# The second layer's z projection by Strassen's form, box sums as jobs through DRAM, and some moved steps

## The chip, the cores and the metric

The kernel runs on one core of a Trainium2 chip. The metric is the device time of one execution in microseconds (us); three runs of the kernel before give a median of 2036.6 (2034.02 to 2039.65). A core has five engines that work from queues of their own, each in order: TensorE (PE, matmuls), VectorE (DVE), ScalarE (ACT), GpSimd (POOL) and SyncE (SP, which only starts transfers). POOL starts transfers too.

## The reference, cut to what matters

Two layers over 1024 tokens of width 1024, with a context of 256 tokens. Layer 0 is a bidirectional mLSTM mixer, layer 1 a grid pooling mixer. Each is: norm, modulate, mixer, norm of the output, gated residual. Layer 1's mixer:

```python
def pool_mixer(h, grid, w_in, w_pool, pool_scale, w_out):
    u, z = jnp.split(h @ w_in, 2, axis=-1)          # 2048 each
    ...
    for g, w in enumerate(POOL_WINDOWS):            # 2, 4, 8, 16
        xg = ug[:, :, g, :]
        ...
        m = box_mean(box_mean(x2, w, 2), w, 1)...   # 16 x 64 grid
        diffs.append(m - xg)
    d = jnp.stack(diffs, axis=2).astype(h.dtype)
    y = jnp.einsum("btgi,gio->btgo", d, w_pool).reshape(bsz, t, D_INNER) * pool_scale
    return (y * jax.nn.silu(z)) @ w_out
```

## The kernel before

Everything lies with features on partitions and tokens along the row. A matrix of weights comes in tiles of 128 output features (`load_w`, L138): SP loads 512 KB, ACT rounds it to a high part, DVE subtracts that for a low part. A product in near full precision is three matmuls per block of 128 inputs (`mm3`, L147: high x high, high x low, low x high), each 128 x 512.

Layer 0 first makes features (`features`, `token_part`, 16 tiles), in which v is formed in small matmuls whose results ACT copies (L415) and, five at a time, casts to a high part (L418) with a low part by DVE before POOL stores both. Then come the z and o tiles in pairs by Strassen's form (`strassen`, inside the block with the T tiles): the pair's weights and the layer input are each cut in 2 x 2 blocks; seven products of four blocks take the place of eight. POOL forms the four weight sums (L574 to L577), ACT and DVE split each product's weights (L584, L585), and DVE combines the results (L593). The sums of the input's blocks were formed earlier (`block_sums`) and lie in DRAM.

The attention heads follow. For the first head SP starts the loads of one x chunk (`start_head`), the gate rows (`load_gates`, L712, L705 asked together with `load_ctx_gates`), the other x chunks (`finish_x`), and the v parts (`fetch_v`); `make_A` and `next_q` form the first q (copied by ACT at L734), and `decay` turns gate rows into exponentials on ACT (L768 to L772).

After the heads come the output product of layer 0 in two halves of 512 tokens (`product`), with a norm of each half as a background job that is advanced by `tick` between the matmuls of other work (`norm0`, `residual`, `next_input`). `squares` lets ACT square a tile and POOL add it (L983); the sum goes through a PE column sum to the norm's factor. `residual` stores its tiles from POOL's queue (L1007).

Layer 1 goes group by group, g = 0 to 3, four u tiles, four z tiles and four pool tiles each. Group 0's u and z tiles run first for half 0, under the norm of half 1, and then for half 1. A u tile's result is copied by ACT twice, into a padded grid U (L1076) and a plain copy (L1077). `box` makes the sums over the window by doubling adds on DVE (L1089, L1093), scales, subtracts (L1097 to L1104), and splits the difference in high and low (L1106, L1107). A z tile gets Silu from PSUM (L1082) and stays in SBUF. A pool tile multiplies four differences by `bw_pool`; DVE scales by `pool_scale` and z (L1158); for groups 0 to 2 POOL stores y to DRAM. In groups 1 to 3 the tiles follow `ORDER_B`, so boxes lie between products. The last product reads y back.

PE's order is written out by hand from ctx1 to the end of group 0's halves, and again for the last product; the order on the other engines and on SP, and PE's order elsewhere, is set by a scheduler that simulates the program. SBUF tiles come from tagged pools: 32 tiles S4 of 4 KB a partition, five T5, six pt of 2 KB, two each of wr, wh, wl (weights raw, high, low). A tile is free again when all that read it, a store to DRAM too, has ended.

Of the kernel before, what the change touches and what calls it, by code (L numbers as in the profile page):

```python
# [51 lines left out]
def hybrid_block(ctx: ExitStack, tc: tile.TileContext, xT, ctxT, vecs, w_ada0, w_ada, w_blk, w_krow, blk_mask, w_gate, w_in, b_gate, w_out,  # L52
# [38 lines left out]
    def f(t):  # L91
        return t.bitcast(F32)
# [39 lines left out]
    x1_d = dr.tile([P, KD, T], F32, name="x1_d")  # L132
    y2_d = dr.tile([12, P, T], F32, name="y2_d")
# [261 lines left out]
    def token_part(n, xmh, xml, xch, xcl):  # L395

        bv = small1([P, 32, 4], "bv", 1)
        V.tensor_tensor(bv, mask, wb[:, 2, n:n + 1].to_broadcast([P, 32, 4]), op=ALU.mult)
        bv = bv.rearrange("p a b -> p (a b)")
        vv = small1([P, 2, 144], "vv", dt=F32R)  # L400
        V.tensor_copy(vv[:, 0, :P], bv)
        V.tensor_tensor(vv[:, 1, :P], bv, f(vv[:, 0, :P]), op=ALU.subtract)
        V.tensor_copy(vv[:, :, P:], f(gm_all[:, n]).rearrange("p (a b) -> p a b", a=2))
        for s0 in (0, 5):
# [12 lines left out]
            V.tensor_tensor(pre[:, s0:s0 + 5], pre[:, s0:s0 + 5], vst[:, 0, :, P:], op=ALU.add)  # L417
            S.activation(vhl[:, 0], vst[:, 0, :, :P], AF.Copy)  # L418
            V.tensor_tensor(vhl[:, 1], vst[:, 0, :, :P], f(vhl[:, 0]), op=ALU.subtract)
            for t, dst in ((vhl[:, 0], vh_d), (vhl[:, 1], vl_d)):  # L420
                nc.gpsimd.dma_start(dst[n // 4, :, s0:s0 + 5, (n % 4) * P:(n % 4 + 1) * P], f(t))
        yield

        gx = gx_all[:, n]
        for ci, (o, w) in enumerate(CHUNKS):
            ch, cl = (xch[0][:, o:o + w], xcl[0][:, o:o + w]) if ci < 2 else (xch[1], xcl[1])
            if n == 0:
                mm(gacc[ci][:32, :w], gx, ch, True, False)
# [106 lines left out]
    with ctx0:  # L535
# [29 lines left out]
        def strassen(src, done):  # L565


            r1, r2 = tl("wr", [P, 8, P]), tl("T5", [P, 8, P])
            nc.sync.dma_start(r1, src[0])
            nc.sync.dma_start(r2, src[1])  # L570
            a11, a12, a21, a22 = r1[:, :4], r1[:, 4:], r2[:, :4], r2[:, 4:]
            s12, s34 = tl("T5", [P, 2, 4, P]), tl("T5", [P, 2, 4, P])
            s1, s2, s3, s4 = s12[:, 0], s12[:, 1], s34[:, 0], s34[:, 1]
            G.tensor_tensor(s1, a21, a22, op=ALU.add)  # L574
            G.tensor_tensor(s2, s1, a11, op=ALU.subtract)
            G.tensor_tensor(s3, a11, a21, op=ALU.subtract)
            G.tensor_tensor(s4, a12, s2, op=ALU.subtract)  # L577
            wt = []

            def product(tag, a, b):  # L580
                i = len(wt) % 2
                wt.append((tl("wh", [P, 2, 4, P], F32R), tl("wl", [P, 2, 4, P], F32R)) if i == 0 else wt[-1])
                hi, lo = (t[:, i] for t in wt[-1])
                S.activation(hi, a, AF.Copy)  # L584
                V.tensor_tensor(lo, a, f(hi), op=ALU.subtract)  # L585
                p = pt_(tag)
                for k in range(4):
                    mm3(p, hi[:, k], lo[:, k], *b[k], k == 0, k == 3)
                return p

            def plus(p, t, d=None):
                d = tl("pt", [P, 512]) if d is None else d
                V.tensor_tensor(d, p, t, op=ALU.add)  # L593
                return d

            p = product("pa", a11, b11)
            p1 = tl("pt", [P, 512])
            S.activation(p1, p, AF.Copy)
            done(0, 0, plus(product("pc", a12, b21), p1))
            u2 = plus(product("pa", s2, tpart(2)), p1, p1)  # L600
            u3 = plus(product("pc", s3, tpart(3)), u2)
            p = product("pa", s1, tpart(1))
            done(1, 1, plus(p, u3))
            plus(p, u2, u2)
            done(1, 0, plus(product("pc", a22, tpart(4)), u3, u3))
            done(0, 1, plus(product("pa", s4, b22), u2, u2))

# [42 lines left out]
        for n in range(0, KE, 2):  # L650
            prod = strassen if n else plain
# [190 lines left out]
    def next_q(cur, tp):  # L842
        return make_q(cur["hd"], cur["A"], tp)
# [150 lines left out]
    def residual(yo, rs, o, w, xr, dst, acc2, engs):  # L994
# [5 lines left out]
        for n in range(8):  # L1000
# [5 lines left out]
            if n % per == per - 1:  # L1006
                nc.gpsimd.dma_start(dst[:, n - per + 1:n + 1, o:o + w], yo[n // per])  # L1007
# [11 lines left out]
    def next_input(x1, rs, hf):  # L1019
        for kp in range(4):  # L1020
            a, b = tl("S4", [P, 2, 512], F32R), tl("S4", [P, 2, 512], F32R)
            h2[hf, kp] = (a, b)
            for j in range(2):
# [4 lines left out]
                V.scalar_tensor_tensor(b[:, j], o, sh1[:, k:k + 1], f(a[:, j]), op0=ALU.add, op1=ALU.subtract)  # L1028
                yield STEP_N
# [31 lines left out]
    def u_start(g):  # L1061
# [4 lines left out]
        U = tl("T5", [P, R_, C_])  # L1066
# [3 lines left out]
        return U, tl("S4", [P, T]), R_, C_, r0, hw  # L1070

    def u_half(ut, w, hf):
        U, ur, R_, C_, r0, hw = ut
        p = pt_("pa")
        h2mm(p, w, hf)
        S.activation(U[:, r0 + 8 * hf:r0 + 8 * hf + 8, hw:], p.rearrange("p (r c) -> p r c", c=64), AF.Copy)  # L1076
        S.activation(ur[:, hf * 512:(hf + 1) * 512], p, AF.Copy)  # L1077

    def z_half(sz, w, hf):
        p = pt_("pc")  # L1080
        h2mm(p, w, hf)
        S.activation(sz[:, hf * 512:(hf + 1) * 512], p, AF.Silu)  # L1082

    def box(ut, g, imv):
        U, ur, R_, C_, r0, hw = ut
        win = WINDOWS[g]
# [18 lines left out]
        a, b = tl("S4", [P, T], F32R), tl("S4", [P, T], F32R)  # L1105
        S.activation(a, ur, AF.Copy)  # L1106
        V.tensor_tensor(b, ur, f(a), op=ALU.subtract)  # L1107
        return a, b

    yraw = {}  # L1110
    for g in range(4):
        imap = tl("T5", [P, T])
        nc.sync.dma_start(imap, inv_cnt[g:g + 1].to_broadcast([P, T]))
        imv = imap.rearrange("p (r c) -> p r c", c=64)
        ut, szs, d = [None] * 4, [None] * 4, []
        if g == 0:
            for hf in range(2):
                for j in range(4):
                    if hf == 0:
                        ut[j] = u_start(g)  # L1120
                    u_half(ut[j], load_w(bw_in[4 * g + j]), hf)
                    if hf:
                        d.append(box(ut[j], g, imv))
                for j in range(4):
                    if hf == 0:
                        szs[j] = tl("S4", [P, T])
                    z_half(szs[j], load_w(bw_in[KE + 4 * g + j]), hf)
                if hf == 0:
                    drain()
            ctx1.close()  # L1130

        def u_tile(j):
            w = load_w(bw_in[4 * g + j])
            ut[j] = u_start(g)
            for hf in range(2):
                u_half(ut[j], w, hf)

        def z_tile(j):
            w = load_w(bw_in[KE + 4 * g + j])
            szs[j] = tl("S4", [P, T])  # L1140
            for hf in range(2):
                z_half(szs[j], w, hf)

        def pool_tile(j):
            n = 4 * g + j
            w = load_w(bw_pool[n], 4)
            for hf in range(2):
                s_ = slice(hf * 512, hf * 512 + 512)
                p = pt_("pb")
                for k in range(4):  # L1150
                    mm3(p, w[0][:, k], w[1][:, k], d[k][0][:, s_], d[k][1][:, s_], k == 0, k == 3)
                if g < 3:
                    o = tl("pt", [P, 512])
# [4 lines left out]
                V.scalar_tensor_tensor(o, p, vc("pool_scale", n), szs[j][:, s_], op0=ALU.mult, op1=ALU.mult)  # L1158
                if g < 3:
                    nc.gpsimd.dma_start(y2_d[n, :, s_], o)  # L1160

        def box_tile(j):
            d.append(box(ut[j], g, imv))

        if g:
            for step in ORDER_B:
                dict(u=u_tile, b=box_tile, z=z_tile, p=pool_tile)[step[0]](int(step[1]))
        else:
            for j in range(4):
                pool_tile(j)  # L1170
# [115 lines left out]
```

## Time and profile before

| what | value |
|---|---|
| median of three runs | 2036.6 us (2034.02 to 2039.65) |
| profiled execution | 2035.27 us, span 2032.8 us |
| PE busy | 1970.0 us, 97% |
| DVE, ACT, POOL busy | 62%, 40%, 25% |
| DMA | 339.47 MB, mean 167 GB/s |
| mean granted clock of PE | 0.992 |

The profiled execution is one run of the program with the hardware profiler; its span goes from the first to the last instruction. Matmuls are pipelined, so two that follow each other overlap in the trace: the time of one is best read from a run of many. Time in which an engine stands still is put down to what released it last.

### The profile page before, as it was taken

What the parts mean: (1) busy time and instruction counts of PE and PEld (TensorE: products, weight loads), DVE (VectorE), ACT (ScalarE), POOL (GpSimd) and SP (SyncE); (2) the same over time, 40 slices, a digit from 0 to 9 for tenths busy, and PEclk for the clock granted to TensorE, in tenths of its full rate; (3) what the DMA queues carried; (4) which work ended last, traced back from release to release, by engine and by line L of the source; (5) the groups of instructions that cost most, each with busy time, mean ns of one, the idle gap of its engine ahead of it and who ended that gap; (6) DMA issues with size and microseconds to landing.
All of it is one profiled execution on the core that took longest, in us unless ns stands there. A gap on an engine that the chain in (4) does not pass through costs nothing.

```text
span 2032.8 us, 26908 instructions
## 1 busy us (share of the span) xinstructions
PE 1970.0 (97%) x10050; PEld 1661.2 (82%) x10050; DVE 1256.6 (62%) x2092; ACT 812.5 (40%) x1357; POOL 500.2 (25%) x682
## 2 busy tenths in 40 slices
PE   6899999999999899999999999999999999999997
PEld 4788888788888688888888878887888888888897
DVE  4777777777767567676576662544747292744444
ACT  5567777433333433323332232533423131224443
POOL 2144334354443111111111101524000000000285
PEclk9999999999999999999999999999999999999998
DMA  9377777854444746446363324534331312133473
GB/s 360 130 259 256 257 258 253 319 167 135 131 150 132 295 148 210 179 140 242 111 232 126 133 70 153 196 113 166 94 114 42 104 52 92 49 114 140 166 272 122
DMA packets 115986, 339.47 MB, mean 167 GB/s; under 512 B 13036, under 2 KB 20716, under 8 KB 115856
## 3 DMA queue, kind: packets, MB, share of 16 engines
q1 hardware_dynamic: 85824, 234.80, 34.2%
q0 software_dynamic: 30032, 102.96, 13.7%
q8 instruction: 78, 1.28, 0.3%
q14 instruction: 52, 0.43, 0.1%
HBM read 234.77 MB, written 102.94 MB: 166 GB/s over the span
## 4 chain that ended last, share of the span: by engine, by line
PE 89%; DMA 3%; ACT 3%; DVE 2%; POOL 2%; issue 1%; SPq 0%; POOLq 0%; DVEq 0%; ACTq 0%
PE pa L136 45%; PE pc L136 34%; PE pb L136 7%; PE pb L795 2%; POOL hn L983 1%; PE pc L826 1%; DVE S L915 1%; DMA S<-in_w_ada_dram 1%; DMA S<-in_ctxT_dram 0%; DMA cst<-in_w_blk_dram 0%; DMA S<-a_d 0%; DMA wr<-in_w_ada_dram 0%; DMA S<-in_xT_dram 0%; POOL S L1003 0%; ACT wh L142 0%
## 5 line engine op out<-in xcount | busy, mean ns | idle before, releaser
L136 PE MATMUL pa<-S,wh 128*128 128x512 f32 (+1 forms) x2448 | 703.5, 372 | 0.0
L136 PEld LDWEIGHTS pa<-S,wh 128*128 128x128 f32 x2448 | 433.9, 189 | 67.7
L136 PE MATMUL pc<-S,wh 128*128 128x512 f32 (+1 forms) x1664 | 465.3, 366 | 1.8 <-DVE wh L721 0.9
L136 PE MATMUL pa<-S,wl 128*128 128x512 f32 (+1 forms) x1224 | 449.9, 368 | 0.1
L136 PEld LDWEIGHTS pc<-S,wh 128*128 128x128 f32 x1664 | 301.3, 189 | 53.4 <-DVE S L915 1.5
L144 DVE TENSOR_TENSOR wl<-wr,wh 128x1024 fp32r<-128x1024 f32 (+1 forms) x124 | 150.2, 1211 | 264.4 <-ACT wh L142 263.2
L136 PE MATMUL pc<-S,wl 128*128 128x512 f32 (+1 forms) x832 | 302.6, 365 | 0.3 <-DVE wl L144 0.2
L142 ACT ACTIVATE wh<-wr 128x1024 fp32r<-128x1024 f32 (+1 forms) x124 | 124.7, 1006 | 365.1 <-PE pc L136 144.4
L136 PEld LDWEIGHTS pa<-S,wl 128*128 128x128 f32 x1224 | 230.5, 188 | 39.8 <-DVE wl L144 0.5
L136 PE MATMUL pa<-S,S 128*128 128x512 f32 (+1 forms) x1152 | 249.6, 363 | 8.0 <-ACT S L734 8.0
L136 PE MATMUL pc<-S,pt 128*128 128x512 f32 x960 | 227.6, 392 | 0.8 <-DVE pt L798 0.5
L136 PEld LDWEIGHTS pa<-S,S 128*128 128x128 f32 x1152 | 192.3, 190 | 37.3 <-ACT S L734 8.6
L136 PEld LDWEIGHTS pc<-S,pt 128*128 128x128 f32 x960 | 178.3, 188 | 37.8 <-DVE S L735 1.0
L136 PEld LDWEIGHTS pc<-S,wl 128*128 128x128 f32 x832 | 157.4, 189 | 26.0 <-DVE wl L144 0.8
L983 POOL TENSOR_TENSOR hn<-hn,pt 128x512 f32<-128x512 f32 (+1 forms) x48 | 75.7, 1578 | 284.4 <-ACT pt L982 283.5
L797 ACT ACTIVATE pt<-pb 128x512 fp32r<-128x512 f32 (+1 forms) x96 | 47.8, 524 | 221.6 <-PE pb L795 221.6
L754 DVE SCALAR_TENSOR_TENSOR T<-pa,T 128x256 f32<-128x256 f32 (+3 forms) x184 | 78.2, 455 | 32.7 <-PE pa L136 31.8
L584 ACT ACTIVATE wh<-T 128x512 fp32r<-128x512 f32 x70 | 41.2, 627 | 96.3 <-PE pc L136 79.5
L136 PE MATMUL pb<-S,wh 128*128 128x512 f32 x256 | 78.9, 389 | 0.0
L415 ACT ACTIVATE T<-pb 128x288 f32<-128x288 f32 x160 | 62.5, 413 | 40.5 <-PE pb L136 33.0
L808 DVE BATCH_NORM_STATS2 st<-pc 128x6 f32<-128x512 f32 x32 | 22.4, 699 | 86.6 <-PE pc L136 86.5
L144 DVE TENSOR_TENSOR wl<-T,wh 128x1024 fp32r<-128x1024 f32 x32 | 45.7, 1428 | 43.4 <-ACT wh L142 43.3
(344 smaller groups left out, 2591.5 us busy)
## 6 DMA issues: line engine op xcount, KB each, us to landing
wr<-in_bw_in_dram SPq DMA_DIRECT2D x40, 512.0 KB, 3.6
wr<-in_w_in_dram SPq DMA_DIRECT2D x34, 512.0 KB, 4.2
wr<-in_w_ada_dram SPq DMA_DIRECT2D x32, 512.0 KB, 4.2
wr<-in_w_out_dram SPq DMA_DIRECT2D x32, 512.0 KB, 3.6
T<-in_bw_out_dram SPq DMA_DIRECT2D x32, 512.0 KB, 4.0
S<-y_d SPq DMA_DIRECT2D x28, 512.0 KB, 7.4
vh_d<-T POOLq DMA_DIRECT2D x32, 320.0 KB, 4.7
vl_d<-T POOLq DMA_DIRECT2D x32, 320.0 KB, 4.5
```

The source lines that it names most:

```text
L136: PE.matmul(out, lhsT, rhs, start=start, stop=stop)
L142: S.activation(h, r, AF.Copy)
L144: V.tensor_tensor(l, r, f(h), op=ALU.subtract)
L415: S.activation(vst[:, :, s - s0], p, AF.Copy)
L584: S.activation(hi, a, AF.Copy)
L754: V.scalar_tensor_tensor(W[:, lo + sh:hi + sh], p[:, lo - o:hi - o], 1.0, W[:, lo + sh:hi + sh], op0=ALU.mult, op1=ALU.mult, accum_out=dp[ ...
L795: PE.transpose(p[:, j], st["M"][:, s * P:(s + 1) * P], ident)
L797: S.activation(th[:, :n], p[:, :n], AF.Copy)
L808: V.bn_stats(b6, pv)
L826: PE.transpose(p[:, c], hn[:, c * P:(c + 1) * P], ident)
L915: V.tensor_tensor(b, yraw[kp, hf], f(a), op=ALU.subtract)
L983: G.tensor_tensor(acc, acc, sq, op=ALU.add)
```

## The change

Layer 1 is put in another order. All 16 u tiles come first: tiles 0 to 7 for half 0 (under the norm of half 1), the same eight for half 1, then tiles 8 to 15 for both. Their results go to DRAM. `box` becomes a job that reads a u tile back, builds U with ACT, and writes the high and low parts of the difference to DRAM. The modulated input without its shift is also stored (by `next_input`), and `block_sums1` reads it back and forms the sums of blocks in the manner of layer 0. Then the z tiles come in eight pairs through `strassen`, which is moved out so that both layers use it (the second weight tile takes an S4 tile here, a T5 tile in layer 0); Silu of z goes to DRAM. The boxes run beside: 0 to 5 beside the first eight u tiles' second half, 6 to 9 beside the others, 10 to 15 beside the first six pairs. The pool products come last, group by group, and read differences and z from DRAM. PE's order is by hand for all of it.

Also moved: the cast of v's parts (a few steps later), the sum of squares (from POOL to DVE), the residual's stores (from POOL's queue to SP's), and the first head's gate loads (after A and the first q).

```diff
         for s0 in (0, 5):
-            vst, vhl = tl("T5", [P, 2, 5, 144]), tl("T5", [P, 2, 5, P], F32R)
+            vst = tl("T5", [P, 2, 5, 144])
             for s in range(s0, s0 + 5):
                 yield
+                if s == 7:
+                    cast(*late)
...
-            S.activation(vhl[:, 0], vst[:, 0, :, :P], AF.Copy)
...
+            late = s0, vst
         yield
+        cast(*late)
...
     cur = start_head(0)
-    cur["R"], cur["rc"] = load_gates(0), load_ctx_gates(0)
     finish_x(cur)
     cur["A"] = make_A(0)
     cur["q"] = next_q(cur, 0)
+    cur["R"], cur["rc"] = load_gates(0), load_ctx_gates(0)
     fetch_v(cur["hd"], 0, 0, 5)
...
             sq = tl("pt", [P, w])
             S.activation(sq, src, AF.Square)
-            G.tensor_tensor(acc, acc, sq, op=ALU.add)
+            V.tensor_tensor(acc, acc, sq, op=ALU.add)
...
-                nc.gpsimd.dma_start(dst[:, n - per + 1:n + 1, o:o + w], yo[n // per])
+                nc.sync.dma_start(dst[:, n - per + 1:n + 1, o:o + w], yo[n // per])
...
+    def u_half(n, w, hf):
+        p = pt_("pc" if n % 2 else "pa")
+        h2mm(p, w, hf)
+        t = tl("pt", [P, 512])
+        S.activation(t, p, AF.Copy)
+        nc.gpsimd.dma_start(u_d[n, :, hf * 512:hf * 512 + 512], t)
...
+    def box(n):
...
+        U, ur = tl("T5", [P, R_, C_]), tl("S4", [P, T])
+        nc.sync.dma_start(ur, u_d[n])
...
+        S.activation(U[:, r0:, hw:], ur.rearrange("p (r c) -> p r c", c=64), AF.Copy)
...
+        a = tl("S4", [P, T], F32R)
         S.activation(a, ur, AF.Copy)
+        nc.gpsimd.dma_start(dh_d[n], f(a))
+        V.tensor_tensor(ur.bitcast(F32R), ur, f(a), op=ALU.subtract)
+        nc.gpsimd.dma_start(dl_d[n], ur)
...
+    for hf in range(2):
+        for n in range(8):
+            u_half(n, load_w(bw_in[n]), hf)
+            if hf:
+                next(sums1, None)
+                if n > 1:
+                    box(n - 2)
+        if hf == 0:
+            drain()
+            sums1 = block_sums1()
...
+    for n in range(8, KE):
+        w = load_w(bw_in[n])
+        for hf in range(2):
+            u_half(n, w, hf)
+        next(sums1, None)
+        if n % 2 == 0:
+            box(n // 2 + 2)
+        if n == 13:
+            load_sums1(2)
+        if n == 14:
+            load_sums1(3)
...
+    def sz_done(n, i, hf, t):
+        S.activation(t, t, AF.Silu)
+        nc.gpsimd.dma_start(sz_d[n + i, :, hf * 512:hf * 512 + 512], t)
+
+    for n in range(0, KE, 2):
+        strassen([bw_in[KE + n + i] for i in range(2)], lambda i, hf, t: sz_done(n, i, hf, t), h2b,
+                 lambda j: [(T1_[j, k][:, 0], T1_[j, k][:, 1]) for k in range(4)], "S4")
+        if n < 12:
+            box(10 + n // 2)
...
     for g in range(4):
+        for k in range(4):
+            pair = [tl("S4", [P, T], F32R) for _ in range(2)]
+            for t, src_ in zip(pair, (dh_d, dl_d)):
+                nc.sync.dma_start(f(t), src_[4 * g + k])
+            d.append(pair)
+        for j in range(4):
             n = 4 * g + j
             w = load_w(bw_pool[n], 4)
             for hf in range(2):
+                sz = tl("pt", [P, 512])
+                nc.sync.dma_start(sz, sz_d[n, :, s_])
...
+    ctx1.close()
```

## Rows read from the trace of the kernel before

**Rows 1.** The page, part 1: busy time, share of the span and instructions of each engine.

```profile
PE 1970.0 (97%) x10050; PEld 1661.2 (82%) x10050; DVE 1256.6 (62%) x2092; ACT 812.5 (40%) x1357; POOL 500.2 (25%) x682
```

**Rows 2.** Waits of PE over the span: total us, times, longest us.

```profile
PE pb L136 <- ACT T L415: 10.8, 9, 2.4
PE pa L136 <- ACT S L734: 8.0, 2, 7.8
PE pb L136 <- POOL hn L983: 6.5, 3, 4.8
```

**Rows 3.** Chain that ended last, in order of time: start us, us, what.

```profile
683.12 6.83 PE pa L136 x24
...
1419.99 5.08 PE pc L136 x12
...
1442.31 21.76 PE pa L136 x96
```

**Rows 4.** Stretches: us, PE, PEld, DVE, ACT, POOL busy (instructions), granted clock, DMA share, GB/s.

```profile
400.00:660.00 260.00, 260.00 (x1149) 215.35 (x1148) 193.92 (x277) 96.40 (x165) 122.93 (x112) 1.00 0.44 143
670.00:695.00 25.00, 16.11 (x77) 13.25 (x76) 12.70 (x28) 15.85 (x25) 3.55 (x8) 0.86 1.04 404
680.00:685.00 5.00, 1.88 (x5) 1.50 (x6) 2.90 (x5) 4.01 (x7) 1.51 (x2) 0.55 1.03 419
1420.00:1425.00 5.00, 5.00 (x13) 3.92 (x14) 0.16 (x1) 0.14 (x1) 1.03 (x1) 0.54 0.00 0
1440.00:1480.00 40.00, 40.00 (x178) 33.12 (x177) 31.09 (x28) 16.79 (x22) 1.11 (x8) 1.00 0.35 105
1480.00:1835.00 355.00, 355.00 (x1568) 294.13 (x1567) 195.78 (x193) 90.35 (x131) 15.51 (x36) 1.00 0.26 86
```

**Rows 5.** Timeline at the first head, SP, ACT, PE: start us, us, engine line operation [idle before].

```profile
658.55 1.01 SPq L712 DMA_DIRECT2D S<-a_d  x2
...
678.44 1.69 ACT L772 ACTIVATE T<-S,cst 128x256 f32<-128x256 f32 x4
...
683.12 1.22 PE L136 MATMUL pa<-S,S 128*128 128x512 f32 x2 [7.85 <-ACT S L734]
```

**Rows 6.** Timeline at the second half's norm, DVE, POOL, PE; columns as in rows 5.

```profile
1394.99 4.87 DVE L1002 TENSOR_TENSOR S<-S,pb 128x512 f32<-128x512 f32 x8
...
1411.88 6.19 POOL L983 TENSOR_TENSOR hn<-hn,pt 128x512 f32<-128x512 f32 x4
...
1418.12 1.86 PE L136 MATMUL pb<-ones,hn 128*128 128x1 f32 x8 [4.84 <-POOL hn L983]
```

**Rows 7.** Timeline in the feature stage, ACT and PE; columns as in rows 5.

```profile
201.15 0.74 ACT L418 ACTIVATE T<-T 128x640 fp32r<-128x640 f32 x1
...
202.24 0.47 PE L136 MATMUL pb<-vv,S 128*128 128x288 f32 x2 [1.14 <-ACT T L415]
```

**Rows 8.** DVE by line, 1425 to 1845: count, busy us, mean ns, idle before.

```profile
L1089 DVE TENSOR_TENSOR T<-T 128x1024 f32<-128x1024 f32 (+6 forms) x40 | 50.4, 1259 | 0.3
L1093 DVE TENSOR_TENSOR T<-T 128x1024 f32<-128x1024 f32 (+7 forms) x40 | 46.5, 1162 | 0.7
L1107 DVE TENSOR_TENSOR S<-S,S 128x1024 fp32r<-128x1024 f32 x16 | 19.6, 1224 | 10.6 <-ACT S L1106 10.6
```

**Rows 9.** DVE and POOL by line and form, 400 to 660; columns as in rows 8.

```profile
L585 DVE TENSOR_TENSOR wl<-T,wh 128x512 fp32r<-128x512 f32 x69 | 47.3, 711 | 0.1
...
L577 POOL TENSOR_TENSOR T<-wr,T 128x512 f32<-128x512 f32 x14 | 23.9, 1710 | 0.0
```

**Rows 10.** DMA: queue (packets, MB, share); one group of issues (count, KB, us to landing).

```profile
q1 hardware_dynamic: 85824, 234.80, 34.2%
...
S<-t_d SPq DMA_DIRECT2D x16, 512.0 KB, 14.5
```

**Rows 11.** Timeline beside POOL's adds, DVE and POOL; columns as in rows 5.

```profile
1312.89 4.39 DVE L144 TENSOR_TENSOR wl<-wr,wh 128x1024 fp32r<-128x1024 f32 x1 [3.78 <-ACT wh L142]
...
1312.39 1.32 POOL L983 TENSOR_TENSOR hn<-hn,pt 128x512 f32<-128x512 f32 x1
```

More of the change, by code (lines that the diff above doesn't have):

```diff
@@ L432, in token_part, with strassen, product, plus @@
                 mm(gacc[ci][:32, :w], gx, ch, False, n == KE - 1)
+    def strassen(src, done, blocks, tpart, tag2):
+        b11, b21, b22 = blocks
+        r1, r2 = tl("wr", [P, 8, P]), tl(tag2, [P, 8, P])
+        nc.sync.dma_start(r1, src[0])
+        nc.sync.dma_start(r2, src[1])
+        a11, a12, a21, a22 = r1[:, :4], r1[:, 4:], r2[:, :4], r2[:, 4:]
+        s12, s34 = tl("T5", [P, 2, 4, P]), tl("T5", [P, 2, 4, P])
+        s1, s2, s3, s4 = s12[:, 0], s12[:, 1], s34[:, 0], s34[:, 1]
+        G.tensor_tensor(s1, a21, a22, op=ALU.add)
+        G.tensor_tensor(s2, s1, a11, op=ALU.subtract)
+        G.tensor_tensor(s3, a11, a21, op=ALU.subtract)
+        G.tensor_tensor(s4, a12, s2, op=ALU.subtract)
+        wt = []
+        def product(tag, a, b):
+            i = len(wt) % 2
+            wt.append((tl("wh", [P, 2, 4, P], F32R), tl("wl", [P, 2, 4, P], F32R)) if i == 0 else wt[-1])
+            hi, lo = (t[:, i] for t in wt[-1])
+            S.activation(hi, a, AF.Copy)
+            V.tensor_tensor(lo, a, f(hi), op=ALU.subtract)
+            p = pt_(tag)
+            for k in range(4):
+                mm3(p, hi[:, k], lo[:, k], *b[k], k == 0, k == 3)
+            return p
+        def plus(p, t, d=None):
+            d = tl("pt", [P, 512]) if d is None else d
+            V.tensor_tensor(d, p, t, op=ALU.add)
+            return d
+        p = product("pa", a11, b11)
+        p1 = tl("pt", [P, 512])
+        S.activation(p1, p, AF.Copy)
+        done(0, 0, plus(product("pc", a12, b21), p1))
+        u2 = plus(product("pa", s2, tpart(2)), p1, p1)
+        u3 = plus(product("pc", s3, tpart(3)), u2)
+        p = product("pa", s1, tpart(1))
+        done(1, 1, plus(p, u3))
+        plus(p, u2, u2)
+        done(1, 0, plus(product("pc", a22, tpart(4)), u3, u3))
+        done(0, 1, plus(product("pa", s4, b22), u2, u2))
     emt = const([P, 8, 36], "emt")
@@ L563, in hybrid_block @@
         b11, b21, b22 = ([h[k + ko, hf] for k in range(4)] for ko, hf in ((0, 0), (4, 0), (4, 1)))
[L565 to L606, printed above, removed]
         def z_done(n, sz, i, hf, t):
@@ new lines, in hybrid_block, with load_sums1 @@
+    for hf in range(2):
[8 more added lines that the diff above has]
+            sums1 = block_sums1()
+    T1_ = {}
+    def load_sums1(j):
+        for k in range(4):
+            T1_[j, k] = tl("S4", [P, 2, 512], F32R)
+            nc.sync.dma_start(f(T1_[j, k]), t1_d[j - 1, k])
+    for n in range(8, KE):
[9 more added lines that the diff above has]
+            load_sums1(3)
@@ new lines, in hybrid_block @@
+    load_sums1(1)
+    load_sums1(4)
+    h2b = [[(h2[hf, k // 2][0][:, k % 2], h2[hf, k // 2][1][:, k % 2]) for k in range(ko, ko + 4)]
+           for ko, hf in ((0, 0), (4, 0), (4, 1))]
+    def sz_done(n, i, hf, t):
[6 more added lines that the diff above has]
+            box(10 + n // 2)
@@ L1110, in hybrid_block @@
     yraw = {}
     for g in range(4):
[L1112 to L1144, printed above, removed]
+        d = []
+        for k in range(4):
+            pair = [tl("S4", [P, T], F32R) for _ in range(2)]
+            for t, src_ in zip(pair, (dh_d, dl_d)):
+                nc.sync.dma_start(f(t), src_[4 * g + k])
+            d.append(pair)
@@ L1157, in pool_tile @@
                     o = yraw[n // 2, hf][:, n % 2]
-                V.scalar_tensor_tensor(o, p, vc("pool_scale", n), szs[j][:, s_], op0=ALU.mult, op1=ALU.mult)
+                V.scalar_tensor_tensor(o, p, vc("pool_scale", n), sz, op0=ALU.mult, op1=ALU.mult)
                 if g < 3:
                     nc.gpsimd.dma_start(y2_d[n, :, s_], o)
[L1162 to L1170, printed above, removed]
+    ctx1.close()
     ctx2 = ctx.enter_context(tc.manual_schedule(engines={mybir.EngineType.PE}))
```

74 lines of the change are left out of this document (49 added, 25 removed).

## Prediction, made before the change was run

> **What bounds the kernel now.** I read the engine totals first: TensorE (PE) is busy 97% of the 2032.8 us span, VectorE (DVE) 62%, GpSimd (POOL) 25% [rows 1]. A share is only an average, so next came the waits of PE: outside the opening loads three causes carry nearly all, ScalarE (ACT) behind the feature copies (10.8 us), ACT at the first attention head (8.0) and POOL at the norms (6.5) [rows 2]. Then the chain of waits, for the price of a matmul: 96 in 21.76 us in layer 1 [rows 3], 0.2267 us each. The stretch table shows the two stages that matter at the clock's upper level (2.4 GHz, granted clock 1.00) with PE busy for the whole of them: layer 0's Strassen stage (260.00 of 260.00) and most of layer 1 (355.00 of 355.00) [rows 4]. So in layer 1 a matmul less is 0.2267 us less, as long as nothing else becomes late. DMA is the resource to watch: it was busy 26% of that stretch [rows 4], and the change sends everything there through DRAM.
>
> **Strassen for z: -21.8 us.** Before, 16 z tiles x 2 halves x 8 blocks x 3 passes = 768 matmuls. After, 8 pairs x 7 products x 4 blocks x 3 passes = 672. 96 fewer x 0.2267 = 21.8 us, all on PE, which sets the end. The u and pool matmuls stay 768 and 384. That the form can run without a gap is seen in layer 0's stage [rows 4].
>
> **The first head: -7 us (0 to -9.2).** PE stands 7.85 us until ACT has copied q; ACT is occupied by decay exponentials until 680.13, which became ready early because the gate rows were asked of SyncE (SP) at 658.55, ahead of six x loads [rows 5]. Then 24 matmuls take 6.83 us [rows 3] where 24 x 0.2267 = 5.44 is normal: the granted clock there is 0.55, near its lower level of 1.2 GHz [rows 4]. Together 9.2. The change puts the four gate loads of SP behind the x loads, A and the first q; behind them on SP stand only the v loads. Next late are the exponentials: six x loads of 0.524 MB at 404 GB/s [rows 4] delay the rows by 7.8 us, the first multiply needs them, and PE can fill three score banks (3 x 12 x 0.2267 = 8.2 us) meanwhile. I take -7.
>
> **Sums of squares on DVE: -8 us (-8.9 to -4).** In the second half's norm PE waits 4.84 us for POOL, whose last four adds take 6.19 us [rows 6]; then 12 matmuls take 5.08 us instead of 2.72 at a granted clock of 0.54 [rows 3, 4]. The other waits for POOL are 6.5 - 4.84 = 1.7 [rows 2]. Together 4.84 + 2.36 + 1.7 = 8.9. On DVE the eight adds cost 8 x 0.61 = 4.9 us (the multiplies before them run at that pitch, 4.87 for 8 [rows 6]): from 1395, three times 4.9 us and two weight splits of 1.22 end near 1412, and PE was there at 1418.12 - 4.84 = 1413.3. Other sums of squares lie beside products of 10.9 us. Residual stores go to SP; queued behind them are weight loads, which run two tiles ahead. I price that at nothing, up to 3 us where a store holds SP in the last product.
>
> **The feature casts: -3.5 us (+2 to -6).** A 0.74 us cast stands just ahead of the copy that PE waits 1.14 us for [rows 7], a pattern that comes four times; the rest of the 10.8 us has other copies ahead of it. The moved casts hold their buffers longer, hence the +2.
>
> **What layer 1 pays on DVE: +4 us (0 to +24).** A box of width w has log2(w) adds in each direction at 1.26 and 1.16 us, and three more operations of 1.22 [rows 8]: 6.1, 8.5 and 10.9 us, and about 14.2 for the widest with its half-size pieces, 158.8 for all sixteen. Strassen has 14 DVE operations a pair at 0.71 [rows 9], 9.9 us. From the second half of the first u tiles (130.6 us) to the end of the z pairs (8 x 84 x 0.2267 = 152.3) PE needs 283 us; DVE needs 16 x 1.22 = 19.5 for weight splits, 32 x 0.71 = 23 for block sums, 158.8 for boxes and 79 for pairs, 280 us. That is 99%, and locally more: 9.9 + 10.9 = 20.8 us in two pairs and 9.9 + 14.2 = 24.1 in four, against 19.04. The cover: a box is wanted only in the pool stage, and from 1440 to 1480 DVE was 78% busy with boxes while PE lost nothing [rows 4]. If that cover is gone, the excess is 2 x 1.8 + 4 x 5.1 = 24 us. I stay near the row of 1440.
>
> **What it pays in DMA: +4 us (0 to +50).** A 512 KB tile is 0.524 MB. In the 130.6 us of u tiles: weights 8.4, u out 6.3 and in 5.2, layer input in 4.2, block sums out and in 16.8, box results out 10.5, maps 1.6: 53 MB. The z pairs move 26 MB in 152 us and leave room. Around the pool products: box results in 16.8, z in 8.4, weights 4.2, y out 6.3 and in 3.1, next weights 1.0, late box and z stores 3.1: 42.9 MB, in 384 x 0.2267 = 87.0 us plus the 16.3 before, in which tiles come free, 103.3. Together 95.9 MB in 233.9 us. A saturated stretch moved 404 GB/s [rows 4]: 237.4 us, +3.5. Over the whole kernel the hardware queue moved 234.8 MB in 34.2% of the span, 338 GB/s while at work [rows 10]: 283.7 us, +49.8. I take the stretch, whose 512 KB tiles resemble these. Under load the block sums of layer 0 took 14.5 us to land [rows 10], so late loads are the form that such a loss takes.
>
> **Joints: +2 us (0 to +6).** The first pair waits for block sums, the last product for y and its split.
>
> **Sum.** -21.8 - 7 - 8 - 3.5 + 4 + 4 + 2 = -30.3 us. The profiled execution took 2035.3 us, 2.5 more than its span and 1.3 below the median of 2036.6: its own sum is 2005.0, on the median 2006.3, so 2006.
>
> **Rivals.**
> - *DVE sets the pace of the z pairs.* For: 99% over the stretch, over 100% in six pairs, in-order queues, and a split that has one product (2.72 us) of time at each pair's start. Against: the boxes of 1440. Price 24 instead of 4: 2026.
> - *POOL holds DVE up.* Beside POOL's adds one weight split of 1.22 us took 4.39 [rows 11], 72% of it lost. Each pair has four POOL adds of 1.3 to 1.7 us [rows 9, 11], 5.9 us; if DVE loses 72% of them in six full pairs, that is 26 us on top of the 24: 2052. Against: layer 0's splits, beside the same adds, average 0.71 [rows 9]. The Trainium skill, "SBUF — State Buffer", section "Who interferes with whom", says that a DVE operation with two SBUF inputs and a GpSimd operation that reads SBUF shut each other out for a whole instruction. The 4.39 agrees, the 0.71 shows little of it.
> - *DMA is the bound* (the slower case). Place: block sums and pool stage. At 338 GB/s it pays 49.8 instead of 4: 2052. Above 350 GB/s it no longer ends slower by 0.3%. For: the whole-kernel figure [rows 10], reads mixed with writes. Against: the 404.
> - *The small moves do not pay* (another wait stands behind each): the 18.5 us go, -21.8 + 10: 2025.
> - *The change does not do what it says:* the few spare S4 and T5 tiles serve both boxes and pairs; if each pair waits one product for a buffer, 8 x 2.72 = 21.8 us, Strassen gains nothing, and with half of the small moves lost too it ends near 2036.
> - *Everything is covered:* -40.3, 1996, the low end of the forecast's own range.
>
> **How the numbers follow.** Forecast 2006, own range 1994 to 2018, full cover included: 0.50. DVE 0.22, small moves 0.10, buffers 0.07, DMA 0.08, POOL 0.03. The range takes in the first three and much of the fourth, 1992 to 2035. A measurement of this kernel can tell about 0.3% (6 us) from no change: faster 0.82, within 0.07, slower 0.11.
>
> **What would show it.** Right: PE busy in every 100 us of layer 1, z matmuls at 0.2267 us, no wait for sums of squares and none above 1 us at the first q, DVE near 95% in the z stage, DMA share near 1.0 in the pool stage with PE still full. Wrong: PE waiting for DVE's low parts in the pairs (DVE, POOL), for landings of box results or weights (DMA), for POOL's block differences (buffers), or a new wait for the exponentials at the first head. It fails as a whole if layer 1's stalls pass 40 us.

## The result and the profile after

The changed kernel takes 2108.41 us (median of 4 runs, 2102.28 to 2112.22) against 2035.31 for the kernel before: ratio 1.0355, 95% interval 1.0322 to 1.0387. It is 73 us slower where 30 us less was predicted. The profiled execution has a span of 2107.7 us, 74.9 more than before.

The page, part 1 (columns as in rows 1):

```profile
PE 1971.7 (94%) x9954; PEld 1655.3 (79%) x9954; DVE 1382.3 (66%) x2269; ACT 838.8 (40%) x1401; POOL 528.0 (25%) x772
```

The 96 matmuls are gone (9954 for 10050), yet PE is busy 1.7 us longer. 96 x 0.2267 = 21.8 us less was due, so 23.5 us of busy time, net over the span, were lost to a slower clock; the other 73.2 us of the longer span are time in which PE stands. The waits of PE (columns as in rows 2) name who it stood for:

```profile
PE pa L142 <- ACT wh L469: 44.1, 6, 30.6
PE pa L142 <- DVE wl L470: 21.6, 8, 3.3
PE pa L142 <- ACT wh L148: 19.1, 1, 19.1
...
PE pa L142 <- DVE T L775: 4.6, 1, 4.6
PE pb L142 <- ACT T L431: 4.1, 4, 2.4
```

L469 and L470 are Strassen's weight splits, L148 that of ordinary weights. The first three rows are new and hold 84.8 us. The rows of the small moves fell as meant: the wait for feature copies (L431, was L415) from 10.8 to 4.1, and POOL's sums of squares (L983 in rows 2) are absent.

Times of the same matmuls place gains and losses. The spread of the second half's norm factor, in layer 1's first u tiles, comes at 1405.54 instead of 1424.90: 19.4 us gained. From there to the end it takes 702.2 us instead of 607.9: 94.3 lost. Stretches of the changed kernel (columns as in rows 4):

```profile
1500.00:1550.00 50.00, 50.00 (x222) 41.40 (x222) 38.76 (x38) 19.26 (x27) 12.09 (x25) 1.00 0.82 298
1550.00:1600.00 50.00, 16.66 (x63) 12.82 (x62) 40.67 (x35) 13.07 (x17) 12.13 (x17) 0.65 0.86 330
...
1800.00:1850.00 50.00, 30.93 (x129) 25.08 (x128) 12.45 (x18) 3.79 (x6) 6.49 (x12) 0.80 0.93 355
```

```profile
1600.00:1750.00 150.00, 124.35 (x488) 98.53 (x487) 129.53 (x146) 50.50 (x78) 47.09 (x61) 0.89 0.36 136
```

The u tiles fill PE. Then three things go wrong: **a seam** ahead of the first z pair, **the pairs** themselves, and **the start of the pool products**. In all three the granted clock also falls (0.65, 0.89, 0.80). Timeline of PE at the three places (columns as in rows 5):

```profile
1592.51 1.22 PE L142 MATMUL pa<-S,wh 128*128 128x512 f32 x2 [30.63 <-ACT wh L469]
...
1644.93 0.73 PE L142 MATMUL pa<-S,wh 128*128 128x512 f32 x2 [2.24 <-ACT wh L469]
1648.99 0.80 PE L142 MATMUL pa<-S,wl 128*128 128x512 f32 x1 [3.33 <-DVE wl L470]
...
1823.49 1.22 PE L142 MATMUL pa<-S,wh 128*128 128x512 f32 x2 [19.07 <-ACT wh L148]
```

*The seam, 30.63 + 2.70 us.* ACT is only the last link. SP and POOL before it:

```profile
1553.22 20.50 SPq L1171 DMA_DIRECT2D S<-t_d  x12
1581.21 0.33 SPq L455 DMA_DIRECT2D S<-in_bw_in_dram  x1
```

```profile
1559.43 1.06 POOL L1151 DMA_DIRECT2D t_d<-S  x2
...
1587.18 0.53 POOL L1132 DMA_DIRECT2D dl_d<-S  x1 [0.73 <-DVE S L1131]
1587.73 1.27 POOL L459 TENSOR_TENSOR T<-S 128x512 f32<-128x512 f32 x1
```

The last block sums are stored only at 1559.43. SP's twelve loads of them hold its queue until 1573.7; behind them r2, the pair's second weight tile (L455), waits 7.4 us more for an S4 tile that a box's store still reads (waits of SP, 1530 to 1600; columns as in rows 2):

```profile
SPq L455 <- DMA dh_d<-S: 7.4, 1, 7.4
```

The tile is asked for at 1581.21, and POOL's first weight sum (L459) comes at 1587.73, behind a box store that waited for DVE.

*The pairs.* Pairs 3 to 6 take 27.2 to 27.3 us each instead of 84 x 0.2267 = 19.04; pair 2 takes 24.7, pair 7 28.2, and pair 8, which has no box beside it, 19.0. One pair's start, on POOL, ACT and DVE:

```profile
1639.16 0.55 POOL L1193 DMA_DIRECT2D sz_d<-pt  x1 [0.84 <-ACT pt L1192]
1639.72 1.31 POOL L459 TENSOR_TENSOR T<-S 128x512 f32<-128x512 f32 x1
...
1642.36 0.56 POOL L1132 DMA_DIRECT2D dl_d<-S  x1
1642.94 1.28 POOL L460 TENSOR_TENSOR T<-T,wr 128x512 f32<-128x512 f32 x1
```

```profile
1644.25 1.15 ACT L469 ACTIVATE wh<-T 128x512 fp32r<-128x512 f32 x2
```

```profile
1643.39 2.03 DVE L1112 TENSOR_TENSOR T<-T 128x1136 f32<-128x1136 f32 x1
1645.35 1.75 DVE L470 TENSOR_TENSOR wl<-T,wh 128x512 fp32r<-128x512 f32 x1
1647.03 1.31 DVE L1112 TENSOR_TENSOR T<-T 128x1120 f32<-128x1120 f32 x1
1648.26 1.28 DVE L470 TENSOR_TENSOR wl<-T,wh 128x512 fp32r<-128x512 f32 x2
```

POOL starts the pair's sums only behind the z stores of the pair before; the third product's sum (L460) ends at 1644.2, and ACT follows. PE had been ready at 1642.69. The low part that PE then waits for (until 1648.99) is the first of the two splits at 1648.26; in DVE's queue a box add, another split and a second box add (L1112) stand ahead of it. DVE is busy 129.53 of 150 us, so the pair looks like a loop through four in-order queues rather than DVE at its limit; b_noadd and b_act below test that.

*The pool start, 19.06 us.* Timeline of SP, and the stretch:

```profile
1775.67 0.33 SPq L1207 DMA_DIRECT2D S<-dl_d  x1
...
1815.78 0.32 SPq L1207 DMA_DIRECT2D S<-dl_d  x1
1817.06 0.33 SPq L146 DMA_DIRECT2D wr<-in_bw_pool_dram  x1
```

```profile
1775.00:1805.00 30.00, 29.42 (x130) 24.03 (x128) 9.18 (x15) 7.12 (x13) 2.71 (x5) 1.00 0.99 379
```

PE waits for weights of the next pool tiles; they are asked for at 1812.55 and 1817.06, behind loads of box results that are wanted only groups later. DMA is full (0.99 of the stretch, 379 GB/s), and each 0.524 MB load then takes 1.28 us in SP's queue (1815.78 to 1817.06): 409 GB/s.

### The profile page after: what moved, and what is told of

The parts are those of the page before. It is cut to its first block, busy times and chain, and to the rows that moved or that the text cites. A ratio compares the mean times of both kernels' runs of the same rounds, so it can differ in the third digit from the quotient of the medians.

```text
span 2107.7 us, 27504 instructions
## 1 busy us (share of the span) xinstructions
PE 1971.7 (94%) x9954; PEld 1655.3 (79%) x9954; DVE 1382.3 (66%) x2269; ACT 838.8 (40%) x1401; POOL 528.0 (25%) x772
## 3 DMA queue, kind: packets, MB, share of 16 engines
q8 instruction: 78, 1.28, 0.2%
## 4 chain that ended last, share of the span: by engine, by line
PE 76%; DMA 8%; DVE 8%; issue 4%; ACT 2%; POOL 1%; SPq 0%; POOLq 0%; DVEq 0%; ACTq 0%
PE pa L142 42%; PE pc L142 29%; PE pb L142 3%; DMA S<-u_d 2%; PE pb L816 1%; DVE T L1112 1%; DVE wl L470 1%; DVE wl L150 1%; DMA wr<-in_w_ada_dram 1%; DMA S<-xh_d 1%; DMA S<-dh_d 1%; DVE S L936 1%; PE pc L847 1%; DMA S<-in_w_ada_dram 1%; DMA S<-in_ctxT_dram 0%
## 5 line engine op out<-in xcount | busy, mean ns | idle before, releaser
L142 PE MATMUL pa<-S,wh 128*128 128x512 f32 (+1 forms) x2576 | 756.0, 378 | 63.1 <-ACT wh L469 44.1
L142 PEld LDWEIGHTS pa<-S,wh 128*128 128x128 f32 x2576 | 464.6, 191 | 140.4 <-ACT wh L469 46.6
L142 PE MATMUL pa<-S,wl 128*128 128x512 f32 (+1 forms) x1288 | 483.9, 376 | 22.2 <-DVE wl L470 21.6
L142 PE MATMUL pc<-S,wh 128*128 128x512 f32 (+1 forms) x1728 | 486.8, 367 | 4.3 <-ACT wh L148 3.3
L150 DVE TENSOR_TENSOR wl<-wr,wh 128x1024 fp32r<-128x1024 f32 (+1 forms) x108 | 124.5, 1152 | 165.0 <-ACT wh L148 164.5
L148 ACT ACTIVATE wh<-wr 128x1024 fp32r<-128x1024 f32 (+1 forms) x108 | 107.6, 996 | 304.9 <-PE pc L142 137.5
L469 ACT ACTIVATE wh<-T 128x512 fp32r<-128x512 f32 x102 | 60.6, 626 | 179.3 <-PE pc L142 150.8
L478 DVE TENSOR_TENSOR pt<-pc,pt 128x512 f32<-128x512 f32 x66 | 45.6, 691 | 75.0 <-PE pc L142 53.7
L470 DVE TENSOR_TENSOR wl<-T,wh 128x512 fp32r<-128x512 f32 x102 | 83.1, 835 | 0.0
L431 ACT ACTIVATE T<-pb 128x288 f32<-128x288 f32 x160 | 63.1, 416 | 41.1 <-PE pb L142 29.1
L478 DVE TENSOR_TENSOR pt<-pa,pt 128x512 f32<-128x512 f32 x88 | 58.4, 684 | 28.7 <-PE pa L142 28.6
```

The source lines that it names most:

```text
L142: PE.matmul(out, lhsT, rhs, start=start, stop=stop)
L148: S.activation(h, r, AF.Copy)
L150: V.tensor_tensor(l, r, f(h), op=ALU.subtract)
```

## The experiments

The first theory: three separate causes (seam by tiles and late sums, pairs by DVE's box adds, pool start by SP's order). Its rivals are that the small moves cost, that POOL's stores delay the pairs, and that one shortage only moves from place to place. Edits are against the changed kernel where nothing else is said.

**s_moves: the small moves alone.** The kernel before with casts, first head's gate loads, squares and residual stores changed, layer 1 left alone.

> The kernel before with the small moves alone: casts of v later, first head's gate loads after A and q, sums of squares on DVE and residual stores on SP. Layer 1 stays as it was. Theory (the small moves do pay): the column sums of the second half's norm come about 19 us earlier, as in the trace of the change, and the whole is 2036.6 - 19 = about 2017 us. Rival (what they give is taken back behind them): within 6 us of the kernel before.

```diff
+    cur["R"], cur["rc"] = load_gates(0), load_ctx_gates(0)
...
-            G.tensor_tensor(acc, acc, sq, op=ALU.add)
+            V.tensor_tensor(acc, acc, sq, op=ALU.add)
```

Measured 2020.18 us (2018.91 to 2021.63) against 2037.11, ratio 0.9919 (0.9905 to 0.9934). The spread of the second norm comes at 1406.73. So the small moves gain 17 us, and layer 1's new form costs 88 (2108.41 - 2020.18).

**b_nobox: no boxes beside the pairs.** Boxes 10 to 15 move into the first two pool groups.

> The changed kernel with boxes 10 to 15 moved out of the z pairs into the first two pool groups. Buffers and queues theory, and DVE theory alike: a pair falls from 27.2 us to its 19.04 us of matmuls, 5 to 6 pairs, some 40 to 45 us less, 2065 us. If a pair still takes 25 us or more, boxes are not what holds the pairs, and it is the stores of z and the weight sums in POOL's own queue. The stall of about 30 us ahead of the first pair stays in either case, since boxes 8 and 9 and the block sums are where they were.

```diff
-        if n < 12:
-            box(10 + n // 2)
...
+            for m in later.get((g, j), ()):
+                box(m)
```

2120.03 us, ratio 1.0408 (1.0392 to 1.0423), far above the 2065 expected. The stretch of the pairs:

```profile
1600.00:1750.00 150.00, 149.01 (x650) 123.09 (x651) 72.00 (x111) 52.15 (x90) 51.05 (x60) 0.99 0.38 130
```

PE is full, so without boxes the pairs run as predicted. But the seam stays (30.27 us), and the late boxes hold the pool products up: 15.98, 5.23, 4.42 and 26.03 us, the first and the last for loads of box results. The loss has moved with the boxes.

**b_noadd: boxes 10 to 15 without the doubling adds** (part of the computation is left out, everything else stays).

> The changed kernel without the doubling adds of boxes 10 to 15 (these box sums are left out; loads, copies, scaling, splits and stores of the six boxes stay). DVE theory: a pair with a box needs some 14.5 us of DVE instead of 20.8 to 24.1, less than its 19.04 us of matmuls, so pairs run at 19 to 20 us: about 2065 us. Queue theory (the pair's weight sums stand behind the box's stores in POOL's order, and the split of a sum behind box work): stalls remain at each pair, 23 us or more a pair, 2085 us or more.

```diff
-        st = 1
+        st = 1 if n < 10 else win
         while st < win:
```

2066.2 us, ratio 1.0155 (1.0138 to 1.0172). In the same stretch:

```profile
1600.00:1750.00 150.00, 145.66 (x634) 119.99 (x633) 102.62 (x128) 60.94 (x98) 58.24 (x72) 0.98 0.60 205
```

With DVE at 68% instead of 86% the pairs run without gaps after one of 4.35 us, while the seam (30.64) and the pool start (18.59) are hardly changed. POOL's first sum of a pair still comes right behind a z store there (1656.49), so that order alone is not the loss. The box adds on DVE are worth 42 us (2108.41 - 2066.2) in the pairs, clock included.

**b_act: stores of z and of the boxes' high parts from ACT's queue** instead of POOL's.

> The changed kernel with the stores of z and of the boxes' high parts started from ACT's queue instead of POOL's. Same work. Queue theory: POOL has only the weight sums, memsets and the low parts' stores left, sums come earlier, a pair falls from 27.2 to about 21 us: 2075 to 2085 us. DVE theory: pairs stay at 24 us or more: 2095 us or more.

```diff
-        nc.gpsimd.dma_start(sz_d[n + i, :, hf * 512:hf * 512 + 512], t)
+        nc.scalar.dma_start(sz_d[n + i, :, hf * 512:hf * 512 + 512], t)
```

2120.48 us, ratio 1.0419 (1.0403 to 1.0435). Pairs 2 to 6 take 23 to 30 us, some 27 on the mean. The z stores on POOL are therefore not what sets them. The seam is longer here (38.51 us) and the wait at the pool start shorter (11.63). The edit does not clear the queue wholly: the low part's store still stands ahead of POOL's sums and waits for DVE:

```profile
1648.41 0.57 POOL L1132 DMA_DIRECT2D dl_d<-S  x1 [21.78 <-DVE S L1131]
1649.00 1.31 POOL L459 TENSOR_TENSOR T<-S 128x512 f32<-128x512 f32 x1
```

**r2_t6: r2 in a T5 tile, six T5 tiles instead of five** (each a little smaller).

> The changed kernel with the second weight tile of a pair in T5 instead of S4, and six T5 tiles of 5440 bytes for five of 5760. Same work on every engine. Buffers and queues theory: the 30.6 us stall ahead of the first pair goes to under 8 us, since its weights no longer wait for a box to give its S4 tile back, and a pair falls from 27.2 to some 20 to 23 us: 2108 - 25 - 20 = about 2063 us. DVE theory (a pair with a wide box needs 24.1 us of DVE): the first stall goes, pairs with wide boxes stay at 24 us or more: about 2080 us. If the first stall stays near 30 us, it is the late block sums that set it, not the tile.

```diff
-    BYTES["T5"] = 5760
+    BYTES["T5"], BUFS["T5"] = 5440, 6
...
-                 lambda j: [(T1_[j, k][:, 0], T1_[j, k][:, 1]) for k in range(4)], "S4")
+                 lambda j: [(T1_[j, k][:, 0], T1_[j, k][:, 1]) for k in range(4)], "T5")
```

2093.64 us, ratio 1.0279 (1.0259 to 1.03). The seam halves (15.71 us, now for the loads of the block sums), the pool start stays (18.40), and the pairs get irregular gaps of up to 16.04 us: r2 and the boxes now share the T5 tiles. Within the longest gap a box's memset on POOL waits 5.32 us for DVE's work on another box (L1125), and the weight sum L460 stands behind it. Neither expectation had this.

**c_order: SP's order in the pool stage written out by hand**, weights and the next group's box results in turn.

> The changed kernel with SP's order in the pool stage written out by hand: weights of two pool tiles and the first group's differences first, then, tile by tile, z, the next weights and one pair of differences of the next group. The same transfers. Theory of the queue's order (28 loads of differences stand ahead of the third pool weight): the 19 us stall at the start of the pool stage goes to under 4 us and no new one above 4 us comes: about 2108 - 18 = 2090 us. Rival (DMA is simply full, 43 MB at about 405 GB/s take 106 us): the stall is spread over the stage, and the time stays within 6 us of the changed kernel's 2108.

```diff
+    ctxs.enter_context(tc.manual_schedule(engines={mybir.EngineType.PE, mybir.EngineType.SP}))
+    w_next = [load_w(bw_pool[n], 4) for n in range(2)]
+    d_all = [load_d(m) for m in range(4)]
```

2092.8 us, ratio 1.0281 (1.0264 to 1.0298). The 19 us at the pool start are gone; four waits of 0.77 to 0.97 us for DMA are left. Seam and pairs do not change (30.62; 2.24 + 3.33 a pair). So that loss was the order of the loads, not the transfer rate: 15.6 us.

**v1_room: r2_t6, with the widest box worked in place**, so that it needs one T5 tile less.

> As the run with the second weight tile in T5 and six T5 tiles, and the widest box works in place instead of in a tile of its own (one DVE operation more, 0.15 us a box), so that a weight tile of the next pair and its sums find room. Buffers theory: the irregular stalls of that run (16.0 and 7.0 us) go, pairs come to 20 to 21 us, about 2065 us; the stall ahead of the first pair stays at about 16 us, because the loads of the block sums set it. DVE theory: pairs at 24 us on the mean, about 2085 us.

```diff
-            M_ = tl("T5", [P, 16, 64])
...
+            V.tensor_tensor(U[:, 0:8, 0:64], U[:, 0:8, 0:64], imv[:, 8:16], op=ALU.mult)
```

2082.2 us, ratio 1.0233 (1.0217 to 1.0248). The pairs:

```profile
1600.00:1750.00 150.00, 138.17 (x595) 111.85 (x593) 145.38 (x169) 60.12 (x97) 66.25 (x68) 0.99 0.49 169
```

Gaps fall to 1.3 to 2.5 us each, and now DVE is near its limit: 145.38 of 150. But box results come late at the pool start (17.46 us), and weights later once more (14.31).

**v3_all: v1_room, block sums advanced twice per u tile, and c_order's queue.**

> As the last, with the block sums given out twice as fast (two steps a tile) and SP's order in the pool stage by hand. If the three losses are separate, the stall ahead of the first pair goes under 5 us, that of the pool stage under 4, and pairs are as in the last run: about 2065 - 14 - 17 = 2034 us. If they are one loss that moves on (DVE or DMA is full over layer 1), the time stays above 2055 us.

```diff
                 next(sums1, None)
+                next(sums1, None)
```

2065.35 us, ratio 1.0151 (1.0134 to 1.0167). v1_room had taken 26 us and c_order 16; with the faster sums they take 43, so the sums added nothing. The seam is still 14.83 us, and the pool start 16.24. SP's timeline tells of the second:

```profile
1733.42 21.04 SPq L146 DMA_DIRECT2D T<-in_bw_out_dram  x5
1754.56 0.38 SPq L1207 DMA_DIRECT2D S<-dh_d  x1
```

Five early loads of the last product's weights wait for T5 tiles that boxes and, for a smaller part, the pairs hold, and the box results that PE needs stand behind them. The rival of one moving shortage gains.

**v4_t1: v3_all with SP's order by hand from the ninth u tile to the last pair.**

> v3_all with one more step: from the ninth u tile to the last z pair SP issues in the order of the code, so that the T1 loads of the block sums no longer stand behind the weights of the second and third z pair. In v3_all they were issued at 1566 us and after, behind a weight load that waited 21 us for its tile, and PE stood 14.83 + 2.08 + 1.04 + 1.26 us for them. If that order is what is left of the loss ahead of the first pair, these waits fall below 5 us in all and the time is near 2050. If the block sums themselves are late (DVE, S4 tiles), PE waits as long for another thing and the time stays above 2060. The wait of about 16 us at the start of the pool stage should stay, since weights of the last product still stand ahead of the d loads there and wait for T5 tiles that boxes hold.

```diff
+    ctxz.enter_context(tc.manual_schedule(engines={mybir.EngineType.SP}))
     for n in range(8, KE):
```

2090.59 us, ratio 1.0257 (1.024 to 1.0274): 25 us slower than v3_all, above 2060 as the second expectation has it. The waits ahead of the first pair for block sums are gone, as the first has it, and so is most of the wait at the pool start, which was expected to stay (2.34 us). But a larger one stands among the u tiles:

```profile
1456.56 25.89 SPq L1105 DMA_DIRECT2D S<-u_d  x5
```

```profile
1516.88 1.22 PE L142 MATMUL pc<-S,wh 128*128 128x512 f32 x2 [39.72 <-ACT wh L148]
```

The loads of five boxes wait 25.89 us for S4 tiles, and u weights stand behind them. In v3_all, where the scheduler orders SP here, no such wait stands among the u tiles.

**v5_late: v4_t1, boxes 12 to 15 in the first pool group**, boxes 10 and 11 beside the first and the third pair.

> v4_t1, but boxes 10 and 11 alone beside the pairs (after the first and the third), and boxes 12 to 15 in the first pool group, whose products need none of them. If DVE's boxes are the cause of the late pairs and, through the T5 tiles that they hold, of the late start of the pool stage, pairs 2 to 8 take 19 to 20 us each, the 16 us gap at the start of the pool stage goes, and the time is 2015 to 2030. If instead the order and number of the transfers hold the pool stage (group 3's d loads now come after late boxes), a gap of 10 us or more stands in the pool stage and the time is above 2040.

```diff
-        if n < 12:
-            box(10 + n // 2)
+        if n in (0, 4):
+            box(10 + n // 4)
...
+            if g == 0:
+                box(12 + j)
```

2134.8 us, ratio 1.0478 (1.0463 to 1.0494). The pairs are nearly full (PE 146.98 of 150 from 1600 to 1750, DVE 100.43), but v4_t1's wait among the u tiles is still there (39.73 us), and PE stands 13.01, 15.44, 12.79 and 24.32 us in the pool stage: three early loads of the last product's weights wait 20 to 22 us each for DVE's work on boxes, and the pool weights and box results stand behind them in SP's queue. The second expectation holds.

**p1_plain: the new order without Strassen's form.** u tiles, boxes through DRAM and pool products as changed; z tiles by eight plain products. No block sums, no sums on POOL, and the 16 S4 tiles of the block sums stay free.

> The changed kernel with its order kept (all u tiles, then all z tiles, boxes as jobs through DRAM, pool products last), but z tiles by eight plain products each instead of Strassen's form: no block sums, no sums on POOL, 16 fewer S4 tiles held. PE then has 174 us of work in the z stage instead of 152. If what Strassen's form asks of DVE, POOL and the tiles is the cause of the loss, the gap of 31 us before the first pair and the gaps of the pairs go, the z stage takes 174 to 178 us instead of 237, the late weights at the start of the pool stage stay, and the time is 2040 to 2055. If the new order and the boxes through DRAM are the cause by themselves, the z stage keeps gaps of 20 us or more and the time stays above 2080.

```diff
-        strassen([bw_in[KE + n + i] for i in range(2)], lambda i, hf, t: sz_done(n, i, hf, t), h2b,
-                 lambda j: [(T1_[j, k][:, 0], T1_[j, k][:, 1]) for k in range(4)], "S4")
+        for i in range(2):
+            w = load_w(bw_in[KE + n + i])
+            for hf in range(2):
+                z_half(n + i, w, hf)
```

2026.2 us (2022.84 to 2026.84), ratio 0.9956 (0.9939 to 0.9973): 82 us faster than the changed kernel with 96 matmuls more, and below the 2040 to 2055 that I gave it. Page part 1, then stretches of the z and pool stages:

```profile
PE 1972.6 (97%) x10050; PEld 1663.2 (82%) x10050; DVE 1292.0 (64%) x2140; ACT 808.3 (40%) x1337; POOL 476.6 (24%) x724
```

```profile
1500.00:1600.00 100.00, 100.00 (x443) 82.81 (x442) 78.37 (x65) 34.56 (x42) 19.11 (x41) 1.00 0.56 203
1600.00:1700.00 100.00, 100.00 (x443) 82.81 (x442) 64.17 (x61) 26.82 (x35) 15.24 (x30) 1.00 0.66 248
1700.00:1800.00 100.00, 95.87 (x416) 78.84 (x416) 27.60 (x39) 12.73 (x21) 16.20 (x30) 0.98 0.83 296
```

From 1404.69 to 1740.34 PE has no gap above 0.5 us. The late weights at the pool start, which I had expected to stay, set no gap. One of 4.12 us is left, for another load: PE waits for DVE's scaling (L1225), and DVE for z, asked for from 1731.91 on, behind loads of box results. With tiles free, the loads of box results start early, from 1673.7 instead of 1751.7. So neither the new order, nor the boxes through DRAM, nor SP's order is slow by itself.

**p2_plain_order: p1_plain with c_order's queue.**

> p1_plain with SP's order of the pool stage written out as in c_order, so that weights and the next group's d loads alternate. If the late weights are the one loss left, the wait of 15 to 19 us at the start of the pool stage goes as in c_order and the time is 2022 to 2035, close to that of the small moves alone (2020.2), since the new order then costs and gives nothing of its own. If the pool stage is bound by the transfers themselves, the time stays above 2040.

```diff
+    w_next = [load_w(bw_pool[n], 4) for n in range(2)]
+    d_all = [load_d(m) for m in range(4)]
```

2022.75 us (2018.98 to 2023.22), ratio 0.9937 (0.9916 to 0.9957). The 4.12 us are gone; one gap of 0.84 is left in the pool stage. It stands within 0.3% of the small moves alone: the new order gives and costs nothing of its own. s_moves, the kernel before with the small moves, stays the fastest (2020.18).

## Why the prediction was wrong

**The cause.** Strassen's form in layer 1 takes 21.8 us of matmuls away and brings 82 us (2108.41 - 2026.2), so it costs about 104 us gross. p1_plain against the changed kernel shows this as a whole; all other code is kept, though the scheduler may order it otherwise. What it brings is several things that wait on each other: block sums and pair operations on DVE and POOL (DVE 1382.3 us busy instead of 1292.0), and 16 S4 tiles held through the z stage. The runs with one cure each show that the loss then moves: cured pairs gave late boxes (b_nobox, v1_room, v5_late), a cured seam gave late weights (v4_t1). The late weights at the pool start are an exception: c_order gained their 15.6 us, and no wait of 1 us or more came up there. How the 104 us divide between tiles and engine time is not settled; no run had Strassen's form with more S4 tiles.

Step by step:

- *Strassen, -21.8 on PE.* The count was right, the condition beside it ("as long as nothing else becomes late") was not met, and a step was missing: each standstill also costs clock, 23.5 us by PE's busy time.
- *DVE, +4 (0 to +24): the step that failed most.* I counted DVE's capacity (99% and an excess of 24 us at most) and took the cover of rows 4, 1440 to 1480. There the box adds lie beside plain products, whose splits run tiles ahead. In a pair, sums, splits and combinations form a chain through POOL, ACT, DVE and PE, and box adds in DVE's queue delay a split that PE wants 2.7 us later. In the changed kernel DVE did not reach its limit (129.53 of 150) and the loss was still 42 us, by b_noadd. The rival with 0.22 named the place and the in-order queues, but priced it by capacity too, at 24.
- *DMA, +4 (0 to +50).* The rate was right: 379 to 409 GB/s against the 404 taken. What I left out is order: weights behind loads that are not yet wanted cost 15.6 us (c_order). I had written that late loads are the form such a loss takes, but priced only bytes.
- *Joints, +2 (0 to +6).* Mis-sized by far: 33.3 us at the seam. The block sums' path (layer input out and in, DVE, store, load) ends late, and then r2 lacks a tile; with a tile for r2, 15.71 us of it stay for the block sums' loads (r2_t6).
- *Buffers.* The rival with 0.07 (one product lost per pair, 21.8 us) named the right resource at the wrong place. One more tile for r2 took away half of the seam (30.63 to 15.71 us, r2_t6). At the pool start the changed kernel's loss was order, by c_order; tiles held the loads up there only in later runs (v3_all, v5_late).
- *POOL holds DVE up.* In part right. DVE by line and form in the changed kernel, 1592 to 1800 (columns as in rows 8):

```profile
L470 DVE TENSOR_TENSOR wl<-T,wh 128x512 fp32r<-128x512 f32 x32 | 35.2, 1112 | 0.0
...
L470 DVE TENSOR_TENSOR wl<-S,wh 128x512 fp32r<-128x512 f32 x8 | 5.4, 678 | 0.0
```

  Splits of POOL's sums take 1112 ns, those that come when POOL is done 678: 32 x 0.434 = 13.9 us of DVE over eight pairs. The mean hides two kinds: in the trace, 9 of the 32 overlap a POOL sum and take 2.22 us on the mean, the other 23 take 0.68. The Trainium skill, "SBUF — State Buffer", section "Who interferes with whom", has the two engines exclude each other, and this row agrees better than layer 0's 711 did. It is no cause by itself: in b_noadd the same splits take 1091 ns and the pairs have no gap.
- *Feature casts, -3.5.* The first q matmul comes 9.0 us earlier (672.37 to 663.34). Mis-sized: 6.7 us of waits for the copies went, where I had counted only the four of which I saw a cast just ahead.
- *First head, -7.* From there to the first norm's column sums only 1.2 us were gained. PE did fill the three score banks, from 665.50 to 673.38, but the last of them is only 256 wide (12 of the 36 matmuls), so the reserve is shorter than the 8.2 us counted; and the multiply that frees the first bank ran only at 677.25, behind its exponentials. PE's timeline in the changed kernel:

```profile
669.62 3.76 PE L142 MATMUL pa<-S,S 128*128 128x512 f32 x19
678.01 11.81 PE L142 MATMUL pa<-S,S 128*128 128x512 f32 x44 [4.63 <-DVE T L775]
```

  The wait for q (7.85) became a wait of 4.63 us for the multiply with the late exponentials, as the prediction named it for "wrong", and 44 matmuls then take 11.81 us instead of 44 x 0.2267 = 9.97.
- *Squares, -8.* Right: 127.86 us from the first norm's column sums to the second's spread became 118.72, -9.1. In the last product a wait for weights of 3.32 us is new (2.58 in s_moves), where SP's stores stand among the weight loads and wait for POOL (four waits, 13.4 us in all); that is slightly above the 3 priced as the most. No run has these stores moved back, so that they cause it is not shown.

Up to the second norm's spread the small moves gave -19.4 for -18.5, so the miss lies in layer 1, and there in stalls of 85 us where the prediction's own limit for failing as a whole was 40.

## What to carry to other kernels

As far as this case shows, a form with fewer matmuls pays only where the engines that feed it have slack at the moment of each split, not on the average, and where its operands fit beside what is in flight; count the chain from the last product of one step to the first split of the next. When a stage is full in tiles, a load that waits for one blocks every load behind it in its queue, so curing one wait uncovers the next. The quickest proof was to keep the new order and take out the clever form: one run told more than the nine with partial cures.

## What the hardware showed that was not expected

A standstill costs more than its length. After the gap of 30.63 us the first two matmuls take 1.22 us, where 0.62 is usual in full stretches, and over 1550 to 1600 the granted clock is 0.65; gaps of 2 to 5 us in each pair keep it at 0.89 from 1600 to 1750. In sum 23.5 us of PE's busy time, a quarter of the 94.3 us lost in layer 1, are matmuls run at the lower clock.
